# Two Strassen products taken together: the high halves of both weight blocks, then the low halves of both

## The chip, the core and the metric

The kernel runs on one core of a Trainium2 chip, as one launch. The metric is the device time of one execution in microseconds (us); lower is better. The engines are named as in the profile: PE is TensorE's matrix array and PEld its weight load, DVE is VectorE, ACT is ScalarE, POOL is GpSimd, SP is SyncE, which here only issues transfers.

## The reference

One layer of an encoder over 512 tokens and 2048 channels, in float32:

```python
u = rms_norm(h, mix_pre_g)
q, k, v, ca, cb, ga, gb = split(u @ w_in)
y_attn = neighbourhood_attention(q, k, v, rpb) @ w_attn_o
y_conv = conformer_conv(ca, cb, ...)
merged = sigmoid(ga) * y_attn + sigmoid(gb) * y_conv
h = h + rms_norm(merged @ w_out, mix_post_g)
u = rms_norm(h, ffn_pre_g)
gate, up = split(u @ w_gate_up)                     # 2048 -> 2 x 5632
h = h + rms_norm((silu(gate) * up) @ w_down, ffn_post_g)   # 5632 -> 2048
```

What matters here are four of its large matrix products: the two gates `ga` and `gb`, `merged @ w_out`, `u @ w_gate_up` and most of `... @ w_down`.

## The kernel before

**Precision.** PE works on rounded float32. A float32 operand is therefore split in two: `hi`, its rounded value, made by ACT (`halved_weights`, line 253), and `lo`, the rest, made by DVE (line 255). A product is the sum hi·hi + hi·lo + lo·hi. An activation block keeps its hi half (256 tokens) in columns A and its lo half in columns B of one 512-wide tile, so that hi weights times all 512 columns and lo weights times the 256 columns A are the three terms: for each product 8 matmuls of 512 columns, then 8 of 256 columns (8, because the inner size is 8 blocks of 128).

**Strassen.** `strassen()` makes two output tiles of 128 x 512 from 2 x 2 blocks with seven products in place of eight. Their operands on the weight side are blocks of the weights (a11, a12, a21, a22, loaded by `quarter`) and sums of them (s1 to s4; s1 is summed by an accumulating transfer from POOL's queue, s2 to s4 by DVE, `wsum`). Three accumulators in PSUM hold the sums: x, y and z. The order of the products on PE is:

1. x = a11 · "11"
2. y = s2 · "T2"
3. z = s1 · "T1"
4. y += s3 · "T3", after DVE has added the copy `p1` of x to y and ACT has copied y to `u2`
5. x += a12 · "21"
6. z += s4 · "22"
7. y += a22 · "T4"

In most calls products 4 and 6 take lo before hi (`turn`), so that runs of one width meet. `strassen()` is called 76 times: 14 calls for the gates (names g2 to g15), 7 for `w_out` (wo0 to wo12), 39 for `w_gate_up` (f5 to f43), and two rounds of 8 for `w_down` (d0 and d1; in the first of them `turn` is off). The first call of each group has `apart` set and puts product 5 into a bank of its own; the other 71 calls have not.

**What orders the work.** A scheduler places the instructions when the kernel is built and fixes one order for each engine; at run time an engine takes its instructions in that order, each waiting for its semaphores. Tiles come from pools that go round: the hi weights have 3 buffers (`whi`), the lo weights 3 (`wlo`). So the cast of the fourth product's hi weights waits until PE has read those of the first, the fifth those of the second, the sixth those of the third. The names in the trace are those of the calls: `g8h` and `g8l` are hi and lo weights of call g8, `g8q` a loaded block, `g8s` a sum, `g8v` the copies `p1`, `u2` and `p5` of PSUM banks (line 280), `g8c` the copies in `done` (line 298).

Some calls have other work beside them: in the `w_gate_up` calls POOL adds squares to a row (`row<-row,asq`, line 953) and scales stored tiles (line 975), in the `w_down` calls it scales outputs (line 1108).

Of the kernel before, what the change touches and what calls it, by code (L numbers as in the profile page):

```python
# [31 lines left out]
P = 128  # L32
NT = 512
# [38 lines left out]
def hybrid_block(ctx: ExitStack, tc, xT, vecs, rpb, mask, w_c0, w_qk, w_v, w_gg, w_cg, w_ao, w_co, w_out, w_g0, w_gu, w_dn, outT):  # L72
    nc = tc.nc
# [11 lines left out]
    HT, HN = KT // 2, NT // 2  # L85
    A, B = slice(0, HN), slice(HN, NT)

    def slot(name, dt=F32, shape=(P, NT)):
        return sp.tile(list(shape), dt, tag="slot", name=name)

    def bank(name):
        return mm.tile([P, NT], F32, tag="mm", name=name)
# [37 lines left out]
    def wraw(name):  # L130
        return wp.tile([P, 1024], F32, tag="raw", name=f"raw_{name}", bufs=5)
# [97 lines left out]
    def operands(b11, b2, t12, t34):  # L229
        return {  # L230
            "11": b11,
            **{n: [t[i] for t in b2] for i, n in enumerate(("21", "22"))},
            **{n: [t[i] for t in t12] for i, n in enumerate(("T1", "T2"))},
            **{n: [t[i] for t in t34] for i, n in enumerate(("T3", "T4"))},
        }

    def sums(w1, name, load=nc.sync.dma_start):

        s1 = stp.tile([P, 1024], F32, tag="S1", name=f"{name}s1")
        load(s1, w1[:, :1024])  # L240
        nc.gpsimd.dma_start(s1, w1[:, 1024:], accum_op=ALU.add)
        return s1

    def quarter(w, c, name, load=nc.sync.dma_start):

        raw = wp.tile([P, 1024], F32, tag="raw", name=f"{name}q", bufs=5)
        load(raw, w[:, c * 1024 : (c + 1) * 1024])
        return raw

    def halved_weights(w, name):  # L250

        hi = wp.tile([P, 1024], F32R, tag="whi", name=f"{name}h")
        nc.scalar.copy(hi, w)
        lo = wp.tile([P, 1024], F32R, tag="wlo", name=f"{name}l")
        nc.vector.tensor_tensor(out=lo, in0=w, in1=hi.bitcast(F32), op=ALU.subtract)
        return hi, lo

    def begun(w0, name):

        a11 = quarter(w0, 0, name)  # L260
        return (a11, *halved_weights(a11, name))

    def strassen(w0, w1, op, name, n, s1=None, behind_last=None, first=None, quarters=None, apart=False, turn=True):

        x, y, z = ((bank, abank)[n % 2](f"{name}_{i}") for i in range(3))

        def wsum(a, b, op, i):
            t = stp.tile([P, 1024], F32, tag="S", name=f"{name}s{i}")
            nc.vector.tensor_tensor(out=t, in0=a, in1=b, op=op)
            return t

        def copied(ps, i):
            t = stp.tile([P, NT], F32, tag="quad", name=f"{name}v{i}", bufs=3)
            nc.scalar.copy(t, ps)  # L280
            return t

        def product(ps, w, b, first=False, last=False, lo_first=False):
            hi, lo = w if isinstance(w, tuple) else halved_weights(w, name)
            ws = [slice(k * P, (k + 1) * P) for k in range(HT)]
            steps = [(hi, slice(0, NT)), (lo, A)]
            if lo_first:
                steps.reverse()
            for n, (wt, cols) in enumerate(steps):
                for k, t in enumerate(op[b]):  # L290
                    nc.tensor.matmul(
                        ps[:, cols], wt[:, ws[k]], t[:, cols], start=first and n + k == 0,
                        stop=last and n + k == HT, skip_group_check=True,
                    )

        def done(ps, i):
            t = stp.tile([P, HN], F32, tag="half", name=f"{name}c{i}", bufs=2)
            nc.scalar.copy(t, ps[:, B])
            return ps[:, A], t

        if quarters:
            a11, a12, a21, a22 = quarters
        elif apart:
            a11, a12, a21, a22 = (first[0], *(quarter(*w, name) for w in ((w0, 1), (w1, 0), (w1, 1))))
        s1 = s1 or sums(w1, name)
        if not apart:
            a11, a21, a12, a22 = (quarter(*w, name) for w in ((w0, 0), (w1, 0), (w0, 1), (w1, 1)))
        product(x, first[1:] if first else a11, "11", first=True)
        if apart:
            v = (bank, abank)[n % 2](f"{name}_3")  # L310
            product(v, a12, "21", first=True, last=True)
        s2 = wsum(s1, a11, ALU.subtract, 2)
        p1 = copied(x, 1)
        product(y, s2, "T2", first=True)
        product(z, s1, "T1", first=True)
        nc.vector.tensor_tensor(out=y, in0=y, in1=p1, op=ALU.add)
        u2 = copied(y, 2)
        s3 = wsum(a11, a21, ALU.subtract, 3)
        product(y, s3, "T3", lo_first=turn)
        p5 = copied(z, 3)  # L320
        nc.vector.tensor_tensor(out=z, in0=z, in1=u2, op=ALU.add)
        if apart:
            nc.vector.tensor_tensor(out=v, in0=v, in1=p1, op=ALU.add)
            x = v
        else:
            product(x, a12, "21", last=True)
        nc.vector.tensor_tensor(out=p5, in0=y, in1=p5, op=ALU.add)
        s4 = s2
        nc.vector.tensor_tensor(out=s4, in0=a12, in1=s2, op=ALU.subtract)
        c11 = done(x, 1)  # L330
        product(z, s4, "22", last=True, lo_first=turn)
        c12 = None if behind_last else done(z, 2)
        product(y, a22, "T4", last=True)
        if behind_last:
            behind_last()
            c12 = done(z, 2)
        return c11, c12, done(y, 3), (p5[:, A], p5[:, B])
# [240 lines left out]
    for h in range(H):  # L578
        bm = bias_of(h)
        qk = []  # L580
        for i in range(2):
            ps = bank(f"qk{h}_{i}")
# [86 lines left out]
    op = operands(b11, b2, t12, t34)  # L669
    for i in range(2, KT):  # L670
        if i > 2:
            s1, quarters = sums(w_cg[2 * CT + KT + 3], "g3", load_in_order) if i == 3 else None, None
        c11, c12, c21, c22 = strassen(
            w_cg[2 * CT + i], w_cg[2 * CT + KT + i], op, f"g{i}", i + 1, s1, quarters=quarters,
            apart=i == 2,
# [3 lines left out]
        if i == KT - 1:  # L679

            for h in range(0, H, 2):
                if h == H // 2:
                    first = wraw("y0_first")
# [106 lines left out]
    for i in (c + n * HT for c in range(HT) for n in range(2)):  # L790
        if i == KT - 1:
            first = begun(w_out[0], "wo0")
# [12 lines left out]
    op = operands(b11, b2, t12, t34)  # L805
    acc = None
    for i in range(0, KT - 2, 2):
        c11, c12, c21, c22 = strassen(
            w_out[i], w_out[i + 1], op, f"wo{i}", i // 2 + 1, first=None if i else first, apart=i == 0
        )  # L810
        for n, halves_of in enumerate((((A, c11), (B, c12)), ((B, c22), (A, c21)))):
            t = slot(f"fo{i + n}")
            for cols, c in halves_of:
                joined(t[:, cols], c)
            nc.scalar.dma_start(f_d[i + n], t)
            acc = sumsq(acc, t, f"f{i + n}")

    last = [slot(f"f{i}") for i in (KT - 2, KT - 1)]
# [3 lines left out]
    for i in range(0, HT, 4):  # L822
        t = stp.tile([P, 4, HN], F32, tag="S1", name=f"m12r{i}")
# [54 lines left out]
    for c in (*range(SPLIT), *range(HT)):  # L878
        if len(u) == 2 * c:
# [3 lines left out]
            cols = A if c < SPLIT else slice(0, NT)  # L883
        else:
            cols = B
# [20 lines left out]
    for j in range(3):  # L906
        t = stp.tile([P, 2, NT], F32, tag="S", name=f"sg{j}")
        t, up = t[:, 0], t[:, 1]
# [10 lines left out]
    for c in range(HT):  # L919
        hi, lo = wchunk(w_g0[1, c], f"f1_{c}")  # L920
        if c == HT - 1:
            first = begun(w_gu[5], "f5")
# [32 lines left out]
    for j in range(2):  # L955
        t = slot(f"sg{3 + j}")
# [5 lines left out]
    op = operands(b11, b2, b_t12, b_t34)  # L962
# [49 lines left out]
    for j in range(5, FT):  # L1012
        if j == FT - 2:
# [4 lines left out]
            first=first if j == 5 else None, apart=j == 5,  # L1018
# [13 lines left out]
        t, up = slot(f"sg{j}"), slot(f"su{j}")  # L1032
# [108 lines left out]
    y = [slot(f"y{o}") for o in range(KT)]  # L1141
# [55 lines left out]
    def halved(n, squares, pin=False):  # L1197

        r = []
        blocks = range(n * NB // 2, (n + 1) * NB // 2)  # L1200
        return (
            lambda: r.append(rstd(squares, D, f"r4{n}", blocks, pin)),
            lambda: r4.insert(0, by_column(r[0], f"r4{n}", blocks, pin)),
        )

    s1, s2 = halved(0, half(0), pin=True)
# [132 lines left out]
```

## Time and profile before

| | |
|---|---|
| median of 3 runs | 2496.39 us (2496.09 to 2500.19) |
| the profiled execution | 2495.9 us, of which the span from first to last instruction is 2494.1 us |
| PE busy | 2471.3 us of the span (99%) |
| DVE busy | 2078.5 us (83%) |
| ACT busy | 1251.1 us (50%) |
| POOL busy | 474.0 us (19%) |
| granted PE clock, mean | 0.997 of full speed |

In the rows of a timeline, matmuls that follow each other with one name are merged into one row: its start is that of the first, and "x8" their number. A PE row's length covers the last matmul's modelled end, which lies beyond the start of the next row; the time that a run takes on PE is therefore read from the start of one row to the start of the next.

### The profile page before, as it was taken

What the parts mean: (1) busy time and instruction counts of PE and PEld (TensorE: products, weight loads), DVE (VectorE), ACT (ScalarE), POOL (GpSimd) and SP (SyncE); (2) the same over time, 40 slices, a digit from 0 to 9 for tenths busy, and PEclk for the clock granted to TensorE, in tenths of its full rate; (3) what the DMA queues carried; (4) which work ended last, traced back from release to release, by engine and by line L of the source; (5) the groups of instructions that cost most, each with busy time, mean ns of one, the idle gap of its engine ahead of it and who ended that gap; (6) DMA issues with size and microseconds to landing.
All of it is one profiled execution on the core that took longest, in us unless ns stands there. A gap on an engine that the chain in (4) does not pass through costs nothing. (4 is left out here: it accounts for less than half of the span.)

```text
span 2494.1 us, 36076 instructions
## 1 busy us (share of the span) xinstructions
PE 2471.3 (99%) x13495; PEld 2147.5 (86%) x13495; DVE 2078.5 (83%) x2743; ACT 1251.1 (50%) x1939; POOL 474.0 (19%) x511
## 2 busy tenths in 40 slices
PE   9999999999999999999999999999999999999997
PEld 7888888888888888889998888888888888888887
DVE  5999897497777658878898888888888889989887
ACT  5223333365556424556455555555555565456553
POOL 0110132130000000021111111122222203532342
PEclk9999999999999999999999999999999999999998
DMA  5246332386667543669456665666666778888886
GB/s 208 96 141 203 106 107 97 117 265 193 195 191 222 179 158 129 201 210 306 141 169 173 182 182 165 184 197 201 213 207 188 226 229 237 240 229 255 225 222 195
DMA packets 165103, 472.89 MB, mean 190 GB/s; under 512 B 18752, under 2 KB 30656, under 8 KB 164928
## 3 DMA queue, kind: packets, MB, share of 16 engines
q1 hardware_dynamic: 109584, 334.02, 39.8%
q0 software_dynamic: 32928, 97.54, 18.2%
q10 hardware_dynamic: 22416, 39.04, 4.2%
q8 instruction: 106, 1.74, 0.3%
q14 instruction: 69, 0.57, 0.1%
HBM read 396.59 MB, written 71.30 MB: 188 GB/s over the span
## 5 line engine op out<-in xcount | busy, mean ns | idle before, releaser
L443 DVE SCALAR_TENSOR_TENSOR cv<-z,vec,cv 128x497 f32<-128x497 f32 (+14 forms) x240 | 190.6, 796 | 4.8
L953 POOL TENSOR_TENSOR row<-row,asq 128x512 f32<-128x512 f32 x30 | 54.1, 1805 | 397.3 <-ACT asq L952 397.3
L1108 POOL TENSOR_TENSOR ys<-ys,row 128x512 f32<-128x512 f32 x32 | 57.7, 1803 | 119.2 <-DVE ys L340 99.3
L143 ACT CAST whi_qk<-raw_qk 128x1024 fp32r<-128x1024 f32 x32 | 33.6, 1051 | 77.1 <-PE qk L193 56.5
L144 DVE TENSOR_TENSOR wlo_qk<-raw_qk,whi_qk 128x1024 fp32r<-128x1024 f32 x32 | 40.5, 1267 | 32.1 <-ACT whi_qk L143 31.9
L143 ACT CAST whi_y<-raw_y 128x1024 fp32r<-128x1024 f32 x31 | 32.6, 1051 | 64.8 <-PE py L193 52.7
L975 POOL TENSOR_TENSOR an<-an,row 128x512 f32<-128x512 f32 x32 | 50.4, 1576 | 74.6 <-DMA an<-a_d 48.5
L742 DVE TENSOR_TENSOR gg<-py,gg 128x512 f32<-128x512 f32 x32 | 21.9, 687 | 46.2 <-PE py L194 43.4
L190 PE MATMUL py<-ycl,whi_y 128*128 128x512 f32 x128 | 49.8, 389 | 0.0
L193 PE MATMUL py<-ych,whi_y 128*128 128x512 f32 x128 | 49.8, 389 | 0.0
L194 PE MATMUL py<-ych,wlo_y 128*128 128x512 f32 x128 | 49.8, 389 | 0.0
L524 POOL TENSOR_TENSOR bm<-braw,msk 128x128 f32<-128x128 f32 x56 | 42.6, 794 | 14.8 <-DMA braw<-in_rpb 14.8
L144 DVE TENSOR_TENSOR wlo_y<-raw_y,whi_y 128x1024 fp32r<-128x1024 f32 x31 | 37.8, 1223 | 9.1 <-ACT whi_y L143 8.7
L451 POOL TENSOR_TENSOR csum<-csum,cv 128x512 f32<-128x512 f32 x7 | 12.7, 1818 | 144.3 <-DVE cv L443 144.3
L173 PE MATMUL f<-b,whi_f 128*128 128x256 f32 x128 | 36.2, 283 | 0.0
L174 PE MATMUL f<-b,wlo_f 128*128 128x256 f32 x128 | 36.2, 283 | 0.0
L172 PE MATMUL f<-b,whi_f 128*128 128x256 f32 x128 | 36.2, 283 | 0.0
L143 ACT CAST whi_ca<-raw_ca 128x1024 fp32r<-128x1024 f32 x12 | 12.6, 1054 | 46.3 <-PE cb L193 18.1
L553 ACT ACTIVATE sc<-sc,st 128x256 f32<-128x256 f32 (+1 forms) x32 | 18.0, 563 | 33.1 <-DVE st L552 33.0
L1109 POOL DMA_DIRECT2D y_d<-ys x32 | 29.4, 919 | 9.4 <-POOL ys L1108 7.8
L769 POOL DMA_DIRECT2D m_d<-m x8 | 4.5, 557 | 136.7 <-ACT m L166 86.3
L575 POOL DMA_DIRECT2D att_d<-ao x8 | 4.4, 555 | 133.5 <-ACT ao L574 112.5
(3250 smaller groups left out, 8797.3 us busy)
## 6 DMA issues: line engine op xcount, KB each, us to landing
raw_qk<-in_w_qk SPq DMA_DIRECT2D x32, 512.0 KB, 3.6
raw_w<-in_w_dn SPq DMA_DIRECT2D x24, 512.0 KB, 5.5
a_d<-sg ACTq DMA_DIRECT2D x44, 256.0 KB, 4.2
raw_v<-in_w_v SPq DMA_DIRECT2D x16, 512.0 KB, 4.4
gg<-g_d SPq DMA_DIRECT2D x32, 256.0 KB, 4.2
raw_y<-in_w_co SPq DMA_DIRECT2D x16, 512.0 KB, 3.6
raw_f<-in_w_g SPq DMA_DIRECT2D x16, 512.0 KB, 4.1
an<-a_d POOLq DMA_DIRECT2D x32, 256.0 KB, 5.8
```

Of the source, the lines that this page charges most:

```text
L143: cast(hi[:, s], raw[:, s])
L144: nc.vector.tensor_tensor(out=lo[:, s], in0=raw[:, s], in1=hi[:, s].bitcast(F32), op=ALU.subtract)
L172: nc.tensor.matmul(o, hi, t[:, B], start=first, stop=False, skip_group_check=True)
L173: nc.tensor.matmul(o, hi, t[:, A], start=False, stop=False, skip_group_check=True)
L190: mmul = nc.tensor.matmul(ps, hi[:, s], al, start=first, stop=False)
L193: nc.tensor.matmul(ps, hi[:, s], ah, start=False, stop=False)
L194: nc.tensor.matmul(ps, lo[:, s], ah, start=False, stop=last)
L443: nc.vector.scalar_tensor_tensor(out=a[:, to], in0=z[:, fr], scalar=col(C_WDW, i * CW + w), in1=a[:, to], op0=ALU.mult, op1=ALU.add)
L524: nc.gpsimd.tensor_tensor(out=bm[:, o + i - i0], in0=raw[:, :, i * BC : (i + 1) * BC], in1=msk[:, o + i - i0, None, :].broadcast_to([P, RO ...
L953: nc.gpsimd.tensor_tensor(out=row[n], in0=row[n], in1=sq, op=ALU.add)
L975: ins = nc.gpsimd.dma_start(t, a_d[DN_P + k]), nc.gpsimd.tensor_tensor(out=t, in0=t, in1=row[k // KT], op=ALU.mult)
L1108: tc.keep_in_program_order(nc.gpsimd.tensor_tensor(out=t, in0=t, in1=row[n], op=ALU.mult))
```

## The change

In calls without `apart` the first two products are issued together: the 8 hi matmuls of x, the 8 hi matmuls of y, the 8 lo matmuls of x, the 8 lo matmuls of y. The copy `p1` of x stands behind them in the code. Nothing is added or left out, and calls with `apart` keep their order.

```diff
+        def half_product(ps, wt, b, cols, start=False, stop=False):
+
+            for k, t in enumerate(op[b]):
+                nc.tensor.matmul(
+                    ps[:, cols], wt[:, k * P : (k + 1) * P], t[:, cols], start=start and k == 0,
+                    stop=stop and k == HT - 1, skip_group_check=True,
+                )
...
-        product(x, first[1:] if first else a11, "11", first=True)
+        w11 = first[1:] if first else halved_weights(a11, name)
         if apart:
+            product(x, w11, "11", first=True)
             v = (bank, abank)[n % 2](f"{name}_3")
             product(v, a12, "21", first=True, last=True)
         s2 = wsum(s1, a11, ALU.subtract, 2)
-        p1 = copied(x, 1)
-        product(y, s2, "T2", first=True)
+        if apart:
+            p1 = copied(x, 1)
+            product(y, s2, "T2", first=True)
+        else:
+
+            wt2 = halved_weights(s2, name)
+            half_product(x, w11[0], "11", slice(0, NT), start=True)
+            half_product(y, wt2[0], "T2", slice(0, NT), start=True)
+            half_product(x, w11[1], "11", A)
+            half_product(y, wt2[1], "T2", A)
+            p1 = copied(x, 1)
         product(z, s1, "T1", first=True)
```

`product` itself now calls `half_product` twice, with the same matmuls as before.

The scheduler gives more than the code moves another place. The rows below are those of call g8; in them names carry numbers: `g8_0`, `g8_1` and `g8_2` are the accumulators x, y and z, `g8s1`, `g8s2` and `g8s3` the sums (s4 is written over s2), `g8v1` is p1, `g8v2` is u2, and `g8v3` is p5.

On PE, where product 3 (z, `g8_2`) ends and product 4 (y, `g8_1`, lo first) begins, before:

```order
3106 L291 MATMUL g8_2_5618<-t126_0_4439,g8l_5676 128x256
3107 L291 MATMUL g8_2_5618<-t127_0_4495,g8l_5676 128x256
3108 L291 MATMUL g8_1_5617<-t340_0_4109,g8l_5701 128x256
3109 L291 MATMUL g8_1_5617<-t341_0_4165,g8l_5701 128x256
3110 L291 MATMUL g8_1_5617<-t342_0_4221,g8l_5701 128x256
```

And with the change, at the same place on PE:

```order
3107 L286 MATMUL g8_2_5618<-t127_0_4495,g8l_5676 128x256
3108 L286 MATMUL g8_0_5616<-b20_0_4094,g8h_5722 128x512
3109 L286 MATMUL g8_0_5616<-b21_0_4150,g8h_5722 128x512
3110 L286 MATMUL g8_0_5616<-b22_0_4206,g8h_5722 128x512
3111 L286 MATMUL g8_1_5617<-t340_0_4109,g8l_5701 128x256
3112 L286 MATMUL g8_1_5617<-t341_0_4165,g8l_5701 128x256
```

Three of the eight hi matmuls of product 5 (x, `g8_0`) now stand between products 3 and 4; the other five follow product 4.

On ACT, from the cast of product 4's hi weights on, before:

```order
425 L253 CAST g8h_5699<-g8s3_5697 128x1024
426 L699 ACTIVATE gb7_5607<-gb7_5607 128x512
427 L280 COPY g8v1_5652<-g8_0_5616 128x512
428 L700 DMA g_d_4046<-gb7_5607 128x512
429 L253 CAST g8h_5722<-g8q_5626 128x1024
430 L280 COPY g8v2_5695<-g8_1_5617 128x512
431 L253 CAST g8h_5746<-g8s2_5650 128x1024
432 L280 COPY g8v3_5719<-g8_2_5618 128x512
```

And with the change, at the same place on ACT:

```order
425 L253 CAST g8h_5699<-g8s3_5697 128x1024
426 L712 ACTIVATE gb7_5607<-gb7_5607 128x512
427 L713 DMA g_d_4046<-gb7_5607 128x512
428 L253 CAST g8h_5722<-g8q_5626 128x1024
429 L280 COPY g8v1_5672<-g8_0_5616 128x512
430 L253 CAST g8h_5746<-g8s2_5634 128x1024
431 L280 COPY g8v2_5695<-g8_1_5617 128x512
432 L280 COPY g8v3_5719<-g8_2_5618 128x512
```

Two things moved: the copy p1 (`g8v1`) now stands behind the cast of a12, and the cast of s4 (`g8h` from `g8s2`) now stands ahead of the copy u2 (`g8v2`), where it stood behind it.

On DVE, from the lo weights of product 3 on, before:

```order
770 L255 TENSOR_TENSOR g8l_5676<-g8s1_5619,g8h_5674 128x1024
771 L340 TENSOR_TENSOR gb7_5607<-g7_1_5433,g7c3_5604 128x256
772 L255 TENSOR_TENSOR g8l_5701<-g8s3_5697,g8h_5699 128x1024
773 L275 TENSOR_TENSOR g9s2_5834<-g9s1_5803,g9q_5806 128x1024
774 L316 TENSOR_TENSOR g8_1_5617<-g8_1_5617,g8v1_5652 128x512
775 L255 TENSOR_TENSOR g8l_5724<-g8q_5626,g8h_5722 128x1024
776 L255 TENSOR_TENSOR g8l_5748<-g8s2_5650,g8h_5746 128x1024
```

And with the change, at the same place on DVE:

```order
770 L255 TENSOR_TENSOR g8l_5676<-g8s1_5619,g8h_5674 128x1024
771 L353 TENSOR_TENSOR gb7_5607<-g7_1_5433,g7c3_5604 128x256
772 L255 TENSOR_TENSOR g8l_5701<-g8s3_5697,g8h_5699 128x1024
773 L255 TENSOR_TENSOR g8l_5724<-g8q_5626,g8h_5722 128x1024
774 L329 TENSOR_TENSOR g8_1_5617<-g8_1_5617,g8v1_5672 128x512
775 L275 TENSOR_TENSOR g9s2_5818<-g9s1_5803,g9q_5806 128x1024
776 L255 TENSOR_TENSOR g8l_5748<-g8s2_5634,g8h_5746 128x1024
```

The lo weights of a12 (`g8l` from `g8q`) moved ahead of the addition y += p1, and the next call's s2 behind it.

Of the 71 calls without `apart`, 44 have these orders on PE and ACT: g3 to g15, wo2, f6 to f22 and f24 to f36. The other 27 (wo4 to wo12, f23, f37 to f43 and all of the d0 and d1 calls) keep u2 ahead of the cast of s4, and products 3 and 4 next to each other; on DVE they take the lo weights of s3, then y += p1, then the lo weights of a12. The orders of POOL's and SP's instructions are the same as before.

## Rows read from the trace of the kernel before

**Rows 1.** The page: share of the span of each engine, and PE's granted clock by slice.

```profile
span 2494.1 us, 36076 instructions
PE 2471.3 (99%) x13495; PEld 2147.5 (86%) x13495; DVE 2078.5 (83%) x2743; ACT 1251.1 (50%) x1939; POOL 474.0 (19%) x511
...
PEclk9999999999999999999999999999999999999998
```

**Rows 2.** Waits of PE: who waited for whom, us in total, times, longest.

```profile
PE py L194 <- DVE wlo_y L144: 1.5, 1, 1.5
PE r_b L367 <- POOL r_r L360: 1.3, 2, 1.0
...
PE g L291 <- DVE g L321: 0.7, 1, 0.7
```

**Rows 3.** Timeline of PE, call g8: start us, length us, engine, line, what.

```profile
649.20 2.00 PE L291 MATMUL g<-b,g8h 128*128 128x512 f32 x8
651.04 1.12 PE L291 MATMUL g<-b,g8l 128*128 128x256 f32 x8
652.00 2.00 PE L291 MATMUL g<-t,g8h 128*128 128x512 f32 x8
...
654.79 2.00 PE L291 MATMUL g<-t,g8h 128*128 128x512 f32 x8
656.63 2.08 PE L291 MATMUL g<-t,g8l 128*128 128x256 f32 x16
658.54 2.00 PE L291 MATMUL g<-t,g8h 128*128 128x512 f32 x8
660.38 1.98 PE L291 MATMUL g<-b,g8h 128*128 128x512 f32 x8
662.20 2.08 PE L291 MATMUL g<-b,g8l 128*128 128x256 f32 x16
...
668.72 0.63 PE L291 MATMUL g<-b,g9h 128*128 128x512 f32 x2
```

**Rows 4.** Timeline of PE, first `w_down` round: first run of two neighbouring calls.

```profile
2129.25 2.00 PE L291 MATMUL d<-d,d_6h 128*128 128x512 f32 x8
...
2148.81 0.40 PE L291 MATMUL d<-d,d_8h 128*128 128x512 f32 x1
```

**Rows 5.** Timeline of ACT and DVE in g8; in brackets idle time and its releaser.

```profile
646.90 1.05 ACT L253 CAST g8h<-g8s 128x1024 fp32r<-128x1024 f32 x1
...
655.06 0.70 DVE L316 TENSOR_TENSOR g<-g,g8v 128x512 f32<-128x512 f32 x1 [0.24 <-PE g L291]
...
655.79 0.59 ACT L280 COPY g8v<-g 128x512 f32<-128x512 f32 x1 [0.70 <-DVE g L316]
...
656.83 1.05 ACT L253 CAST g8h<-g8s 128x1024 fp32r<-128x1024 f32 x1 [0.45 <-PE g L291]
...
657.78 0.59 ACT L280 COPY g8v<-g 128x512 f32<-128x512 f32 x1
657.91 1.23 DVE L255 TENSOR_TENSOR g8l<-g8s,g8h 128x1024 fp32r<-128x1024 f32 x1 [1.03 <-ACT g8h L253]
...
659.05 0.69 DVE L321 TENSOR_TENSOR g<-g,g8v 128x512 f32<-128x512 f32 x1
```

**Rows 6.** Timeline of the first gate call, g2, where PE waits for u2.

```profile
540.91 0.69 DVE L316 TENSOR_TENSOR g<-g,g2v 128x512 f32<-128x512 f32 x1
...
541.63 0.59 ACT L280 COPY g2v<-g 128x512 f32<-128x512 f32 x1 [0.23 <-DVE g L316]
...
542.27 1.22 PE L291 MATMUL g<-t,g2l 128*128 128x256 f32 x8 [0.28 <-ACT g2v L280]
...
543.33 2.00 PE L291 MATMUL g<-t,g2h 128*128 128x512 f32 x8
```

**Rows 7.** Timeline of POOL and DVE in f10, and in f36.

```profile
1359.95 2.00 PE L291 MATMUL f<-b,f10h 128*128 128x512 f32 x8
...
1364.46 1.22 DVE L275 TENSOR_TENSOR f11s<-f11s,f11q 128x1024 f32<-128x1024 f32 x1
1364.48 2.36 POOL L953 TENSOR_TENSOR row<-row,asq 128x512 f32<-128x512 f32 x1 [15.75 <-ACT asq L952]
...
1873.60 1.29 POOL L953 TENSOR_TENSOR row<-row,asq 128x512 f32<-128x512 f32 x1 [12.81 <-ACT asq L952]
1873.64 2.32 DVE L275 TENSOR_TENSOR f37s<-f37s,f37q 128x1024 f32<-128x1024 f32 x1
```

More of the change, by code (lines that the diff above doesn't have):

```diff
@@ L281, in copied @@
             return t
+        def half_product(ps, wt, b, cols, start=False, stop=False):
[4 more added lines that the diff above has]
+                )
         def product(ps, w, b, first=False, last=False, lo_first=False):
             hi, lo = w if isinstance(w, tuple) else halved_weights(w, name)
-            ws = [slice(k * P, (k + 1) * P) for k in range(HT)]
             steps = [(hi, slice(0, NT)), (lo, A)]
@@ L289, in product @@
             for n, (wt, cols) in enumerate(steps):
[L290 to L294, printed above, removed]
+                half_product(ps, wt, b, cols, first and n == 0, last and n == 1)
         def done(ps, i):
```

## Prediction

> **What bounds the kernel now.** I read the page first: PE is busy for 99% of the span, at a granted clock of 2.4 GHz (9 in every slice but the last, which reads 8), while DVE has 83% and ACT 50% [rows 1]. A busy PE may still be a waiting one, so I read PE's waits next: the longest are single ones of 1.5 us, and inside the Strassen calls the largest is one of 0.7 us [rows 2]. PE's own order and pace therefore set the time. An edit gains only by making the matmuls follow each other faster, and loses by any wait that it brings to PE. In the 76 calls PE hardly waits, but what it does not wait for comes from a chain of DVE and ACT steps whose slack has to be read call by call.
>
> **What the regrouping itself is worth.** It moves matmuls and removes none. In g8 a run of eight hi matmuls takes 1.84 us behind a lo run (649.20 to 651.04) and 1.82 us behind another hi run (660.38 to 662.20); sixteen lo matmuls take 1.91 us, so eight take 0.95 to 0.96 [rows 3]. Entering a hi run from a lo run thus costs some 0.02 us. A second look gives the same: g8 enters a hi run five times and lasts 19.52 us from its first matmul to that of g9 [rows 3], d_6 in the first `w_down` round has the same matmuls, enters seven times and lasts 19.56 us [rows 4]; 0.04 us for two. One entry saved in all 71 calls would be 71 x 0.02 = 1.4 us, 0.06% of the time.
>
> But 44 of the 71 calls do not save it: there three hi matmuls of product 5 now stand between products 3 and 4, and the call enters a hi run five times as before. So the gain is 27 x 0.02 = **-0.5 us**.
>
> **What the other engines' order costs.** I follow g8 with T = 0 at its first matmul, and the durations of [rows 3]. x hi runs to 1.84, y hi (1.82) to 3.66, x lo to 4.61, y lo to 5.57, z hi (1.84) to 7.41, z lo to 8.36. The early need of y's hi weights is covered: the cast of s2 began at 646.90 and took 1.05 us, over a microsecond ahead of T = 0 [rows 5], and it is now needed at T = 1.84. The three filler matmuls of product 5 end at 8.36 + 3 x 0.23 = 9.05. Then comes product 4, which may write y only when ACT has copied it (u2).
>
> When is u2 done? The cast of s4 now stands ahead of it on ACT. That cast needs the buffer of z's hi weights, and so starts 0.20 us behind the start of z's lo run (656.63, 656.83 [rows 3, 5]): T = 7.41 + 0.20 = 7.61. The next ACT instruction starts 0.95 us later (656.83 to 657.78 [rows 5]): u2 at 8.56, with its 0.59 us done at 9.15. In g2, the one gate call where PE did wait for u2, PE went on 0.05 us after the copy's end (541.63 + 0.59 = 542.22, then 542.27 [rows 6]). So product 4 starts at 9.20 in place of 9.05: 0.15 us late. In g2 the eight lo matmuls after the wait took 1.06 us (542.27 to 543.33 [rows 6]) in place of 0.95, another 0.11. **0.26 us** for each call with this order. Queued behind the s4 cast is u2 alone, and behind u2 DVE's z += u2, which is needed by product 6 some 5 us later.
>
> Is u2's input ready by 8.56? DVE's lo weights of s3 now wait for x's lo run, which ends later. DVE follows the end of a PE run by 0.27 us (654.79, 655.06 [rows 3, 5]): 4.61 + 0.27 = 4.88. Lo weights take 1.14 us from their start to the next instruction's (657.91 to 659.05 [rows 5]): the lo weights of a12 at 6.02, the addition to y at 7.16, done at 7.86. That is 0.70 us early; it costs nothing in g3 to g15, wo2 and f21.
>
> In the other 29 of the 44 (f6 to f20, f22, f24 to f36) POOL adds a row of squares. In f10 that instruction starts at T = 1364.48 - 1359.95 = 4.53 [rows 7], 0.35 us before DVE's lo weights of s3 can now start. In f36 POOL was first by 0.04 us: it took 1.29 us, and DVE's instruction beside it 2.32 in place of 1.23, ending 1.07 us after POOL's [rows 7]. In f10 DVE was first by 0.02 us and POOL took 2.36 [rows 7]. So whoever comes second waits. Placing POOL at 4.53 to 5.82, the lo weights of s3 end at 5.82 + 1.07 = 6.89, as if begun at 5.66; a12's begin at 6.80, the addition at 7.94 and ends at 8.64. ACT follows by 0.03 us (540.91 + 0.69 = 541.60, then 541.63 [rows 6]): u2 at 8.67 in place of 8.56. **0.37 us** for each of these calls.
>
> The Trainium skill (SBUF — State Buffer, section "Who interferes with whom") has a rule that speaks against such a move: a VectorE instruction with two SBUF inputs and a GpSimd one that reads SBUF exclude each other, and the first to start blocks the other for its whole length. By that, taken strictly, the lo weights of s3 would begin at 5.82 rather than as if at 5.66, each of the 29 calls would lose 0.53 us, and the time would be 2515 us; the trace agrees on who waits, and I take its 1.07 us.
>
> In the 27 calls without filler u2 is ahead of the s4 cast: lo weights of s3 at 4.88, the addition at 6.02 to 6.72, u2 from 6.75 to 7.34, product 4 at 8.36. A microsecond of slack hides the later start, even with a POOL instruction of 1.29 us across most of it. Nothing is charged there, and a slip of 0.2 us in some of them would be a few microseconds at most.
>
> **The sum.** 15 x 0.26 + 29 x 0.37 - 0.5 = 3.9 + 10.7 - 0.5 = +14.1 us on the profiled execution's 2495.9 us (its span is 2494.1): **2510 us**. The median of the runs shown, 2496.39, is 0.5 us above that execution. Differences within 0.2%, 5 us, are about what a measurement here can't tell from no change.
>
> Bounds of what the rows of before don't show. The wait of 0.15 us is a difference of times that I trust to some 0.05 us, and the restart of 0.11 us is one example: with 0.10 and no restart, 44 x 0.10 - 0.5 = 3.9, or 2500 us. On the upper side DVE's lo weights of s3 could take the whole 2.32 us of f36 from 4.88: they end at 7.20, u2 starts at 8.98, 0.42 late, each of the 29 loses 0.68 us, and the sum is 19.7 + 3.9 - 0.5 = 23, or 2519 us.
>
> **The rivals.**
>
> *No wait at all (not slower).* If u2 ends by 9.00 in place of 9.15, the filler covers it, and what is left is the saved entries: 2495.4 us. It decides at 0.15 us, a sixth of the s4 cast that stands in front. For it: the margin is small, and three matmuls are in place to cover it. Against it: every step comes from a row of this kernel and the sum has no free term; POOL only makes it later. It would also be so if ACT could take u2 while the s4 cast waits; then u2 could run from 7.89 on. The Trainium skill (PSUM — Partial Sum Buffer, section "Engine vs sequencer instructions") says that ScalarE's queue is strictly first in, first out; no run here shows the opposite, so I leave this rival at 12%.
>
> *DVE is the bound in the f calls.* The forced pause until 4.88 costs DVE up to 1.5 us of each 19.5, at 83% busy on the mean [rows 1]. If POOL's other instructions also lengthen a12's lo weights by 1.09 us (2.32 - 1.23 [rows 7]) in the 14 later of these calls, u2 slips by about that much: 14 x 1.09 = 15 us more, 2525 us. It decides once the addition to y ends behind T = 8.53. For it: that margin is already used up in the sum. Against it: POOL works for 19% of the span [rows 1], and its queue holds the other instructions behind transfers. 15%.
>
> *The regrouping pays in all calls.* -1.4 us, 2494.5 us: it needs no wait and no filler, and even then stays below what can be told. 3% for anything faster by over 0.2%, this one included.
>
> **How the numbers follow.** The waits as summed have 70% (2502 to 2515), no wait 12%, DVE as bound 15%, faster 3%. Slower by over 0.2%: the first and third, with a little of the first lying below the bound and counted as same: 0.85. Within 0.2%: 0.12. Faster: 0.03. The range reaches from the lower bound to just above the upper one, 2500 to 2520 us, and leaves out most of rivals one and two and the faster case.
>
> **What would show it.** In the changed trace PE should wait about 0.15 to 0.3 us for ACT's copy, once in each of the 44 calls and at product 4, and the period of a g call should be 19.78 us in place of 19.52, that of f6 to f36 some 19.9. In wo4 to wo12, f37 to f43, d0 and d1 the period should be 0.02 us shorter and without a wait. The prediction is wrong if PE's waits at product 4 are missing, if they are released by DVE's lo weights of s3 rather than by the copy, or if waits turn up at products 6 or 7.

## The result and the profile after

The changed kernel takes **2509.49 us** (median of 6 runs, 2506.77 to 2510.40); the kernel before takes 2496.66 us beside it (6 runs, 2495.84 to 2500.19). The ratio is 1.0048, with a 95% interval of 1.0037 to 1.0058: slower by about 13 us, where 2510 was forecast.

The page of the profiled execution (2509.41 us), beside [rows 1]:

```profile
span 2507.6 us, 36110 instructions
...
PE 2481.1 (99%) x13495; PEld 2143.6 (85%) x13495; DVE 2063.3 (82%) x2743; ACT 1246.0 (50%) x1939; POOL 461.8 (18%) x511
...
PEclk9999999999999999999999999999999999999998
```

PE's busy time grew by 10 us and its share stayed at 99%: the page hides the waits, as the prediction warned ("A busy PE may still be a waiting one"). The clock is the same. The loss has to be read from starts.

The timeline of PE, DVE and ACT in g8, which answers to [rows 3, 5]; the call begins at 650.82, so T is the time less that. The copy row marked x2 holds u2 and, behind it, p5:

```profile
650.82 2.00 PE L286 MATMUL g<-b,g8h 128*128 128x512 f32 x8
...
654.47 1.11 PE L286 MATMUL g<-b,g8l 128*128 128x256 f32 x8
...
655.43 1.12 PE L286 MATMUL g<-t,g8l 128*128 128x256 f32 x8
655.70 1.23 DVE L255 TENSOR_TENSOR g8l<-g8s,g8h 128x1024 fp32r<-128x1024 f32 x1 [2.14 <-PE g L286]
...
657.98 0.69 DVE L329 TENSOR_TENSOR g<-g,g8v 128x512 f32<-128x512 f32 x1
...
658.23 1.12 PE L286 MATMUL g<-t,g8l 128*128 128x256 f32 x8
658.43 1.05 ACT L253 CAST g8h<-g8s 128x1024 fp32r<-128x1024 f32 x1 [2.06 <-PE g L286]
...
659.18 0.86 PE L286 MATMUL g<-b,g8h 128*128 128x512 f32 x3
659.39 1.06 ACT L280 COPY g8v<-g 128x512 f32<-128x512 f32 x2
...
660.01 1.00 PEld L286 LDWEIGHTS g<-t,g8l 128*128 128x128 f32 x8 [0.41 <-ACT g8v L280]
660.01 1.21 PE L286 MATMUL g<-t,g8l 128*128 128x256 f32 x8
...
661.06 1.32 PE L286 MATMUL g<-t,g8h 128*128 128x512 f32 x5
```

Step by step: z's lo run starts at T = 7.41, the cast of s4 at 7.61, u2 at 8.57. The filler starts at 8.36, and product 4 at 660.01, T = 9.19. Its lo run then takes 1.05 us (to 661.06) in place of 0.95. DVE's addition is done at 658.67, T = 7.85, 0.7 us ahead of the copy. PE's row shows no idle time ahead of product 4, but the row of its weight load does: PEld waited, and ACT's copy released it. DVE idles 2.14 us for x's lo run, which costs nothing here.

The timeline of f10, where POOL adds its row (answers to [rows 7]; T = 0 at 1364.89):

```profile
1364.89 2.00 PE L286 MATMUL f<-b,f10h 128*128 128x512 f32 x8
...
1369.42 1.29 POOL L966 TENSOR_TENSOR row<-row,asq 128x512 f32<-128x512 f32 x1 [16.16 <-ACT asq L965]
...
1369.77 2.03 DVE L255 TENSOR_TENSOR f10l<-f10s,f10h 128x1024 fp32r<-128x1024 f32 x1 [1.54 <-PE f L286]
...
1372.30 1.11 PE L286 MATMUL f<-t,f10l 128*128 128x256 f32 x8
1372.56 1.05 ACT L253 CAST f10h<-f10s 128x1024 fp32r<-128x1024 f32 x1 [1.86 <-PE f L286]
1372.86 0.69 DVE L329 TENSOR_TENSOR f<-f,f10v 128x512 f32<-128x512 f32 x1
...
1373.58 1.08 ACT L280 COPY f10v<-f 128x512 f32<-128x512 f32 x2
1374.22 1.21 PE L286 MATMUL f<-t,f10l 128*128 128x256 f32 x8
```

DVE's lo weights of s3, second to POOL, take 2.03 us and end 1.09 us behind it; the addition to y ends at T = 8.66, u2 starts at 8.69, product 4 at 9.33. But look at the cast: it starts 0.26 us behind z's lo run (1372.30), not 0.20 as in g8. Even with no POOL, ACT could not have taken u2 before T = 7.67 + 0.95 = 8.62, with the 0.95 us of [rows 5] from a cast's start to the next instruction's.

Periods (first matmul of a call to that of the next), as the difference between the two profiled executions; in us:

| calls | forecast per call | measured per call | forecast sum | measured sum |
|---|---|---|---|---|
| g3 to g15, wo2, f21 (15) | +0.26 | +0.22; f21 +0.28, g15 +0.25 | +3.9 | +3.4 |
| f6 to f20, f22 (16) | +0.37 | f7 to f20 +0.35 to +0.37, f6 +0.29, f8 +0.56, f22 +0.28 | +5.9 | +5.7 |
| f24 to f36 (13) | +0.37 | +0.29, f25 +0.34 | +4.8 | +3.9 |
| the other 27 | -0.02 | -0.02, with a few strays | -0.5 | -0.4 |

Together +12.6, of a span that is 13.5 us longer; calls with `apart` and the stretches between the groups hold the rest.

### The profile page after: what moved, and what is told of

The parts are those of the page before. It is cut to its first block, busy times and chain, and to the rows that moved or that the text cites. A ratio compares the mean times of both kernels' runs of the same rounds, so it can differ in the third digit from the quotient of the medians.

```text
span 2507.6 us, 36110 instructions
## 1 busy us (share of the span) xinstructions
PE 2481.1 (99%) x13495; PEld 2143.6 (85%) x13495; DVE 2063.3 (82%) x2743; ACT 1246.0 (50%) x1939; POOL 461.8 (18%) x511
## 5 line engine op out<-in xcount | busy, mean ns | idle before, releaser
L966 POOL TENSOR_TENSOR row<-row,asq 128x512 f32<-128x512 f32 x30 | 38.6, 1287 | 405.7 <-ACT asq L965 405.7
L143 ACT CAST whi_ca<-raw_ca 128x1024 fp32r<-128x1024 f32 x12 | 12.6, 1053 | 46.3 <-PE cb L193 18.1
L1051 DVE TENSOR_TENSOR sg<-sg,su 128x512 f32<-128x512 f32 x39 | 30.0, 770 | 0.0
```

The lines of the kernel that those rows point to most:

```text
L143: cast(hi[:, s], raw[:, s])
L966: nc.gpsimd.tensor_tensor(out=row[n], in0=row[n], in1=sq, op=ALU.add)
```

## The experiments

The state of things at this point: every call with the new ACT order loses at product 4, and the sizes are right within 0.1 us per call, but for f8. Two theories had to be told apart. **Mine:** two gates stand ahead of product 4. ACT's is the cast of s4, which waits for z's hi run and has u2 queued behind it; DVE's is the lo weights of s3, which wait for x's lo run and now have a12's lo weights ahead of the addition. The later one decides. **The rival:** only ACT's order matters, so putting u2 first again is the cure; or, the other way, the regrouping itself is the loss.

In the edits `issued_behind(a, b)` has the scheduler place instruction a behind instruction b on their engine. Lines that only keep the instructions by name, or set the same buffer count elsewhere, are left out ("..."). Rows of the first three experiments carry somewhat higher line numbers, since their kernels have a few lines more.

**1. u2 ahead of the cast again, in all 71 calls, nothing else.**

```diff
...
+        wt4 = halved_weights(s4, name)
+        if not apart:
+            issued_behind(casts[-1], copies[2])
-        product(z, s4, "22", last=True, lo_first=turn)
+        product(z, wt4, "22", last=True, lo_first=turn)
```

> The changed kernel with one edge added: ACT takes the copy u2 ahead of the cast of s4 in all calls, as before the change. DVE keeps the changed order (lo weights of a12 ahead of y += p1). In g4 to g14 the scheduler then puts products 3 and 4 next to each other, as in all f calls. Theory, two gates one behind the other (the s4 cast on ACT, and the late addition on DVE): the first gate is gone, the second now decides without a filler to cover it. The addition ended at T = 7.85 in g8 of the changed kernel, so u2 is done at 8.47, PE goes on at 8.52 in place of 8.36: 0.16 late, 0.1 for the restart, 0.02 saved, about +0.24 us on the period of before (19.51) in the g calls; in the 29 f calls with POOL's row addition the addition ends near 8.65, PE goes on near 9.3: about +1.0 us each. Sum about 12 x 0.24 + 29 x 1.0 = 32 us, some 2528 us. Rival, the s4 cast ahead of u2 is the only cause: all waits vanish, 2495 to 2496 us. Rival, the loss is in splitting product 5 on PE: the filler is gone here, so also 2495 to 2496 us.

Measured: 2530.67 us (4 runs; before 2496.97), ratio 1.0135 (1.0122 to 1.0149). Opening one gate made it worse by 21 us. The filler is gone, so product 4 is due at T = 8.36, and DVE's gate, which had been covered, is not. f10 (T = 0 at 1367.50):

```profile
1367.50 2.00 PE L288 MATMUL f<-b,f10h 128*128 128x512 f32 x8
...
1375.46 0.69 DVE L331 TENSOR_TENSOR f<-f,f10v 128x512 f32<-128x512 f32 x1
...
1376.24 0.59 ACT L282 COPY f10v<-f 128x512 f32<-128x512 f32 x1 [2.94 <-DVE f L331]
...
1376.87 1.22 PE L288 MATMUL f<-t,f10l 128*128 128x256 f32 x8 [0.85 <-ACT f10v L282]
```

ACT stood idle for 2.94 us waiting for DVE's addition (T = 7.96 to 8.65), PE for 0.85 us behind it. f6 to f20 and f24 to f36 lose 1.01 to 1.09 us each, the gate calls 0.29: there the addition ends at T = 7.85, the copy at 8.52.

**2. Both gates opened:** as experiment 1, and the addition to y ahead of a12's lo weights and of the next call's s2.

```diff
...
+        if not apart:
+            issued_behind(sums_of[2], adds[-1])
...
+            wt5 = halved_weights(a12, name)
+            issued_behind(lows[-1], added_y)
-            product(x, a12, "21", last=True)
+            product(x, wt5, "21", last=True)
...
```

> The changed kernel with both orders put back: on ACT u2 ahead of the s4 cast, on DVE y += p1 ahead of the lo weights of a12 and of the next call's s2, in all 71 calls. The regrouped hi and lo matmuls stay. Theory of two gates: with both open no wait is left (in the f calls u2 ends near T = 8.15, PE needs it at 8.36), and all 71 calls keep the saved entry of 0.02 us: 1.4 us under before, about 2495.2 us, period 19.49 us in g3 to g15, wo2 to wo12 and f6 to f43. Rival, the regrouping itself costs (x's lo buffer is released 1.8 us later, whatever the order): waits remain, and the time stays over 2500 us. Rival, the saved entry is worth nothing: 2496.5 us, period 19.51.

Measured: 2495.13 us (11 runs), ratio 0.9989 (0.9980 to 0.9998). All calls but a few strays have a period of 19.49 us, 0.02 less than before. f10 (T = 0 at 1358.96):

```profile
1358.96 2.00 PE L288 MATMUL f<-b,f10h 128*128 128x512 f32 x8
...
1363.49 1.28 POOL L976 TENSOR_TENSOR row<-row,asq 128x512 f32<-128x512 f32 x1 [15.81 <-ACT asq L975]
...
1363.84 2.02 DVE L257 TENSOR_TENSOR f10l<-f10s,f10h 128x1024 fp32r<-128x1024 f32 x1 [1.53 <-PE f L288]
...
1365.79 0.69 DVE L333 TENSOR_TENSOR f<-f,f10v 128x512 f32<-128x512 f32 x1
1366.37 2.08 PE L288 MATMUL f<-t,f10l 128*128 128x256 f32 x16
...
1366.51 0.59 ACT L282 COPY f10v<-f 128x512 f32<-128x512 f32 x1 [1.75 <-DVE f L333]
```

POOL delays DVE here exactly as in the changed kernel (2.02 us), and it costs nothing: the copy ends at T = 8.14, 0.22 us ahead of product 4, and the lo runs of products 3 and 4 are one run of 16. So the regrouping itself is not the loss; it gains what [rows 3, 4] said, 0.02 us per call. This is the best version, 0.11% faster than before, less than one can rely on.

**3. The kernel before, without the regrouping, with the cast of s4 ahead of u2 in all 71 calls.**

```diff
...
+        wt4 = halved_weights(s4, name)
+        if not apart:
+            issued_behind(copies[2], casts[-1])
-        product(z, s4, "22", last=True, lo_first=turn)
+        product(z, wt4, "22", last=True, lo_first=turn)
```

> The kernel before the change, with one edge added: ACT takes the cast of s4 ahead of the copy u2 in all 71 calls. Products 1 and 2 are not regrouped, and DVE adds p1 to y early, as before. The scheduler puts three matmuls of product 5 between products 3 and 4 here too. Theory: the s4 cast ahead of u2 is enough for the wait by itself, whatever the order of products 1 and 2: product 3's lo run starts at T = 7.43, the cast at 7.63, u2 at 8.58 and done at 9.17, PE goes on at 9.22 in place of 9.07 behind the three matmuls; with the restart and one more entry into a hi run about +0.24 us in each of 71 calls, and no more in the f calls than in the g calls, since DVE is early: +17 us, about 2513 us. Rival, the regrouping (the late lo buffer) is the cause and the order on ACT only goes with it: no wait, 2496 to 2498 us.

Measured: 2518.25 us (4 runs), ratio 1.0083 (1.0067 to 1.0098), +21.3 us summed over the periods, of which 1.6 stand in the first call of the second `w_down` round, whose ACT order the edit does not touch. Gate calls lose 0.25, f calls 0.29 to 0.31, whether POOL adds in them or not, most others 0.26 to 0.31. ACT's order alone makes the loss, filler included, in calls that the change left alone too; I had put the price of the f calls 0.06 too low. g8 (T = 0 at 650.44):

```profile
650.44 2.00 PE L293 MATMUL g<-b,g8h 128*128 128x512 f32 x8
...
656.30 0.70 DVE L318 TENSOR_TENSOR g<-g,g8v 128x512 f32<-128x512 f32 x1 [0.24 <-PE g L293]
...
658.07 1.05 ACT L255 CAST g8h<-g8s 128x1024 fp32r<-128x1024 f32 x1 [1.74 <-PE g L293]
658.82 0.86 PE L293 MATMUL g<-b,g8h 128*128 128x512 f32 x3
659.02 1.07 ACT L282 COPY g8v<-g 128x512 f32<-128x512 f32 x2
...
659.66 1.22 PE L293 MATMUL g<-t,g8l 128*128 128x256 f32 x8
```

Cast at T = 7.63, u2 at 8.58, product 4 at 9.22: the changed kernel's picture, without its regrouping. DVE's addition is done at 6.56 here, long before ACT comes to u2, so DVE's gate has no part in it.

**4. The change without POOL's row addition.** It leaves out the addition of the squares to the rows, and with them their sums.

```diff
-                nc.gpsimd.tensor_tensor(out=row[n], in0=row[n], in1=sq, op=ALU.add)
```

> The changed kernel without POOL's additions of squares to the two rows in the w_gate_up calls (the rows then hold one square each; ACT still makes the squares). Orders on PE, ACT and DVE stay as in the changed kernel. Theory: the excess of the f calls over the g calls (0.35 in f7 to f20 and 0.29 in f24 to f36, against 0.22 in g4 to g14, all over the periods of before) is POOL's instruction standing before DVE's lo weights of s3; without it the f calls fall to +0.22: 14 x 0.13 + 13 x 0.07 and a little for f8, about 3 us less, 2506 to 2507 us. Rival, the excess comes from ACT's square or its transfer issue ahead of the a12 cast: the periods of the f calls stay at +0.29 to +0.35, 2509 us.

Measured: 2507.87 us (4 runs), ratio 1.0042 (1.0028 to 1.0056). f7 to f20 fall from +0.35 to +0.28 or +0.29 (f8 stays at +0.56); f24 to f36 stay at +0.27 to +0.29. I expected +0.22 in all of them, as in the gate calls: half wrong. f25 falls from +0.34 to +0.29. So POOL costs 0.05 to 0.08 us in 14 calls (f7, f9 to f20 and f25), 1 us in all, and at most 0.02 us in each of the others. This is read from the periods; the two medians, 1.6 us apart, would not show it by themselves. What keeps the f calls 0.07 above the gate calls is the cast's later start on ACT, which was in this trace and in the one of before, and which I had not looked at in an f call.

**5. The change with four buffers for the hi weights in place of three** (and 64 in place of 66 slots for other tiles). Is it the order on ACT, or what the cast in front waits for?

```diff
...
-        hi = wp.tile([P, 1024], F32R, tag="whi", name=f"{name}h")
+        hi = wp.tile([P, 1024], F32R, tag="whi", name=f"{name}h", bufs=4)
...
```

> The change with 4 buffers in place of 3 for the hi weights (and 64 in place of 66 slots for other tiles, to make room). The cast of s4 still stands ahead of u2 on ACT in all calls, and ahead of p1 too, but it now needs the buffer of y's hi weights, free at T = 3.65, in place of z's, free at 7.41. No filler stands between products 3 and 4 except in g3 and g15, and DVE adds p1 to y ahead of the lo weights of a12. My theory (the price is the wait of that cast for its buffer, with everything behind it on ACT, not the order of the names): the cast runs from about 3.9 to 4.9, the addition ends at 6.7 (7.5 beside POOL), u2 by 8.2, product 4 starts at 8.36 unhindered, every call is 0.02 us shorter than before the change: 2495 us. Rival (a cast ahead of the copy always costs, or POOL's row of squares makes the addition too late by itself): 0.2 to 0.3 us in each call or in the 29 calls with POOL's addition, 2502 to 2512 us.

Measured: 2497.86 us (10 runs; before 2496.28), ratio 1.0003 (0.9993 to 1.0013). 62 of the 71 calls, f7 to f36 with it but for f23, have a period 0.02 us shorter than before. f10 (T = 0 at 1361.86):

```profile
1361.86 2.00 PE L286 MATMUL f<-b,f10h 128*128 128x512 f32 x8
...
1365.71 1.05 ACT L253 CAST f10h<-f10s 128x1024 fp32r<-128x1024 f32 x1 [0.23 <-PE f L286]
...
1367.94 0.69 DVE L329 TENSOR_TENSOR f<-f,f10v 128x512 f32<-128x512 f32 x1
...
1368.65 0.59 ACT L280 COPY f10v<-f 128x512 f32<-128x512 f32 x1 [1.40 <-DVE f L329]
1369.27 2.08 PE L286 MATMUL f<-t,f10l 128*128 128x256 f32 x16
```

The cast of s4 is still ahead of u2, but runs at T = 3.85, behind y's hi run, and product 4 follows product 3 at once. So a cast in front of the copy costs nothing by itself; with experiment 3, the price is the wait of that cast for its buffer. The buffer moved DVE's order too: the addition now stands ahead of a12's lo weights, so this run opens both gates, as experiment 2 does by hand. The time missed its 2495 us outside these calls. In the profiled execution PE is 0.5 us behind the kernel before at 184 us of that kernel's span and 3.7 us behind at 233 us, in the matrix product `pv`, ahead of all Strassen calls; experiment 7, which has the 64 slots alone, loses nothing there. Why that happens with the fourth buffer is open.

**6. The change with four buffers for the lo weights** (and 64 slots).

```diff
...
-        lo = wp.tile([P, 1024], F32R, tag="wlo", name=f"{name}l")
+        lo = wp.tile([P, 1024], F32R, tag="wlo", name=f"{name}l", bufs=4)
...
```

> The change with 4 buffers in place of 3 for the lo weights (and 64 in place of 66 slots for other tiles). DVE's lo weights of s3 no longer wait for x's lo run; those of a12 do. In the gate and w_out calls the scheduler now puts u2 ahead of the cast of s4: 0.02 us shorter than before the change. In f6 to f22, f24 to f36 and one more the cast stays ahead of u2, with the filler, and the lo weights of a12 ahead of the addition. My theory: there ACT's gate alone decides, with its cast at T = 7.66, and POOL costs nothing: +0.29 us in each, also in f7 to f20, where the change costs 0.35; 31 x 0.29 - 40 x 0.02 = +8 us, 2505 us. Rival (POOL's row of squares still delays DVE's addition by blocking the lo weights of a12 in place of those of s3): +0.35 in f7 to f20, 2506 us; rival (DVE's pause until 4.88 was the cause of it all): -0.02 in all calls, 2495 us.

Measured: 2521.60 us (4 runs), ratio 1.0099 (1.0084 to 1.0114). In the calls that it was meant for it went as expected: g3 to g15 -0.02, f6 to f22 and f24 to f36 +0.27 to +0.30 with no difference between early and late ones (f19 strayed to +0.57, and wo2, where the cast stayed in front, lost 0.23). f10 (T = 0 at 1361.99):

```profile
1366.52 2.35 POOL L966 TENSOR_TENSOR row<-row,asq 128x512 f32<-128x512 f32 x1 [16.04 <-ACT asq L965]
...
1367.64 2.32 DVE L255 TENSOR_TENSOR f10l<-f10q,f10h 128x1024 fp32r<-128x1024 f32 x1
...
1369.65 1.05 ACT L253 CAST f10h<-f10s 128x1024 fp32r<-128x1024 f32 x1 [1.86 <-PE f L286]
1369.88 0.69 DVE L329 TENSOR_TENSOR f<-f,f10v 128x512 f32<-128x512 f32 x1
...
1370.61 1.07 ACT L280 COPY f10v<-f 128x512 f32<-128x512 f32 x2
1371.24 1.22 PE L286 MATMUL f<-t,f10l 128*128 128x256 f32 x8
```

The addition ends at T = 8.58, u2 starts at 8.62, as ACT's cast allows: POOL makes DVE wait by a microsecond and the call loses 0.29 all the same. What I did not expect are the `w_down` calls, +0.96 to +1.09 in 11 of the 14 without `apart`, 11.4 us of the miss; f23, f39 and f42 add 3.2. There u2 stands ahead of the cast, no filler covers, and DVE has the next call's s2 and a12's lo weights ahead of the addition: the pattern of experiment 1. That order is not enough by itself. g3 to g15, f40 and f41 of this run have it too and keep -0.02: in f40 the addition ends at T = 7.48. What the losing calls have besides is a POOL instruction that lengthens one of DVE's ahead of the addition by about 1 us. d_6 of the first round (T = 0 at 2144.42):

```profile
2148.57 1.63 POOL L1121 TENSOR_TENSOR ys<-ys,row 128x512 f32<-128x512 f32 x1
2148.80 2.48 DVE L275 TENSOR_TENSOR d_8s<-d_8s,d_8q 128x1024 f32<-128x1024 f32 x1
...
2151.21 1.21 DVE L255 TENSOR_TENSOR d_6l<-d_6q,d_6h 128x1024 fp32r<-128x1024 f32 x1
...
2152.34 0.68 DVE L329 TENSOR_TENSOR d<-d,d_6v 128x512 f32<-128x512 f32 x1
2153.06 0.59 ACT L280 COPY d_6v<-d 128x512 f32<-128x512 f32 x1 [3.25 <-DVE d L329]
...
2153.70 2.12 PE L286 MATMUL d<-d,d_6h 128*128 128x512 f32 x8 [0.76 <-ACT d_6v L280]
```

The next call's s2 takes 2.48 us behind POOL's instruction, where it takes 1.23 in g8 of this run, and the addition ends at T = 8.60, u2 is done at 9.23 and product 4 starts at 9.28, where it was due at 8.36.

**7. The kernel before with 64 slots**, the control of experiments 5 and 6.

```diff
-    sp = ctx.enter_context(tc.tile_pool(name="sp", bufs=66))
+    sp = ctx.enter_context(tc.tile_pool(name="sp", bufs=64))
```

> The kernel before with 64 in place of 66 slots for other tiles, as in the two runs with a fourth buffer, to see what the two slots are worth by themselves. Expected: no change, 2496.5 us, all periods as before within 0.02 us. Rival: loads start later and PE waits for them here and there, some us more; then the two other runs have to be read against this one.

Measured: 2499.86 us (10 runs), ratio 1.0012 (1.0003 to 1.0021): the rival, not the expectation. The Strassen calls without `apart` keep their periods; g2, wo0 and d_0 of the second round, the first of their groups, are 1.6 to 2.1 us longer, though g2 also begins 1.3 us earlier, and the last of the three strays in other runs too (see the end). Against this control experiment 5 is 2.0 us faster by the medians; since it loses its time at another place, that difference is not the gain of the calls.

## Why the prediction was right, point by point

**The saved entries** were right: -0.02 us per call wherever nothing waits, 19.513 to 19.493 us, in 22 of the 26 calls whose period can be read, and in nearly all 71 of experiment 2.

**ACT's order** was right step by step. Forecast for g8: cast 7.61, u2 8.56, product 4 at 9.20. Measured: 7.61, 8.57, 9.19. The restart, taken from the one example in [rows 6] as 0.11, is 0.10 (1.05 us for the lo run in place of 0.95). The term of 0.26 us came out at 0.22 by the period. The unrounded starts of g8's matmuls place it: 0.135 us of wait and 0.097 of restart, less 0.013, since the three filler matmuls pay less for entering a hi run (0.017 us) than the eight would have (0.028); the sum is 0.219, so splitting product 5 costs nothing beyond the wait and the restart. Experiments 3 and 5 show that the wait of the cast is the cause: the order on ACT alone, without the regrouping, brings the loss, and with an earlier buffer the cast may stay in front, once DVE is early as well. The Trainium skill (PSUM — Partial Sum Buffer, section "Engine vs sequencer instructions") has ScalarE take its instructions strictly in order. The trace agrees in experiment 3: in g8 the input of u2 was ready at T = 6.56, ACT stood idle until 7.63, and u2 still started only at 8.58, behind the cast. In the changed kernel g8 can't tell: its cast had begun at 7.61, before u2's input was ready at 7.85. So the prediction's other way out, u2 running from 7.89 while the cast waits, was not one: by its own times the cast no longer waited then, and held ACT until 8.56.

**POOL's term is the one that was mis-sized**, with the right sum for a partly wrong reason. The step "ACT follows by 0.03 us: u2 at 8.67 in place of 8.56. 0.37 us for each of these calls" gave POOL 0.11 us in 29 calls, 3.2 us. The times were right (u2 at T = 8.69, product 4 at 9.33 in f10), but 8.56 was the wrong time to compare with: in an f call the cast starts 0.26 us behind z's lo run, not 0.20, so u2 could not have begun before 8.62. Of the 0.11, then, some 0.06 is ACT's in all 30 f calls with this order, f21 too, and 0.07 POOL's in f7, f9 to f20 and f25 alone; that makes some 2.8 us in place of 3.2, and that it comes so near is luck. In the others of f24 to f36 POOL's addition begins some 0.07 us earlier (T = 4.46 in f30 against 4.53 in f10), and the addition ends in time for ACT: nothing. The cast's 0.25 us stood in the trace of f10 before the change; I had read it in g8 only.

**DVE behind POOL.** The forecast end of s3's lo weights, T = 6.89, is 6.91 in f10. The Trainium skill (SBUF — State Buffer, section "Who interferes with whom") has the second of the two blocked for the whole length of the first. On who waits the trace agrees; on how long it differs: DVE ended 1.09 us behind POOL's end where it takes 1.23 alone, so the sum by the strict rule, 2515 us, was too high.

**The 27 calls** were right: a microsecond of slack hid the later lo weights, but for a stray of +0.15 us in d_4 of the first `w_down` round and the saved entry that f23 does not show.

**The rivals.** No wait at all fell: product 4 starts 0.14 us behind the filler's end in the gate calls, 0.2 in most of f24 to f36 and 0.27 in f10, and later than that end in all 44. DVE as the bound fell for this kernel, but DVE's gate and ACT's lie within some 0.07 us of each other in the f calls where POOL's row comes first; experiment 1 shows what stands behind it, 1.0 us per call, as soon as ACT's gate and the filler are gone. In the `w_down` calls of experiment 6 the rival's mechanism is seen at work: POOL lengthens a DVE instruction by about 1 us, the addition slips, and the call loses as much. That the regrouping pays in all calls is true of experiment 2, where both orders were put right, and it then pays about what the prediction said, 0.02 us per call.

**What would show it.** The periods did, and so does the list of waits of the weight loads (PEld): in each of the 44 calls product 4's first weight load waits for u2's copy, 0.41 us in the gate calls, 0.46 to 0.54 in the f calls, 0.74 in f8. In the trace of before only g2, f5 and d_0 of the second round have such a wait. These times count from the end of the weight load before, and so are longer than what PE lost. The list of PE's own waits shows little: the modelled end of the filler's last matmul covers most of the wait, and of the 44 I found a row in f8 alone, which lost most:

```profile
1334.48 1.22 PE L286 MATMUL f<-t,f8l 128*128 128x256 f32 x8 [0.31 <-ACT f8v L280]
```

So "PE should wait about 0.15 to 0.3 us, once in each of the 44 calls" is right in fact; the place to read it is PEld, not PE.

## What to carry to other kernels

Before a regrouping on the engine that bounds is priced by its own matmuls, look at when each tile's buffer now comes free and what the scheduler does on the other engines with that: here 0.02 us per call was to be had and 0.2 to 0.37 was lost to a cast that stood in front of a copy and waited for its buffer. Several gates can stand ahead of one matmul, and only the last shows as a wait, so price the second before opening the first: undoing one alone cost 21 us more, undoing both gave the gain. Read each step's delay in one call of every group, not in one call for all, and look for short waits of PE in the rows of its weight loads.

## What the runs showed of the hardware that I had not expected

- **A cast with one more semaphore instruction ahead of it starts later.** The cast of s4 waits for PE's semaphore alone in g8, and for PE's and one of ACT's own in f10; the trace has one more semaphore instruction on ACT's queue there. The cast starts 0.20 us behind the start of z's lo run in g8 and 0.26 in f10, and the same stands in the trace of before, 0.20 [rows 3, 5] and 0.25 (f10, 1367.38 to 1367.63). The Trainium skill (Perfetto Trace Analysis, section "Identifying Dependency Chains") says that an instruction which waits for several engines may have semaphore instructions put ahead of it, and the trace agrees. No run varied the wait alone, so that it is the cause of the 0.06 us is argued, not shown. The rows of f10 before the change:

```profile
1367.38 2.08 PE L291 MATMUL f<-t,f10l 128*128 128x256 f32 x16
...
1367.63 1.05 ACT L253 CAST f10h<-f10s 128x1024 fp32r<-128x1024 f32 x1 [0.50 <-PE f L291]
```

- **f8** has that extra instruction at the same T = 7.61, and its cast only at 7.94, 0.28 later than in f10, both in the changed kernel and, by its +0.56, in experiment 4. What delays it is open.
- **The first call of the second `w_down` round** differs from that of before by -0.5 to +1.6 us from profile to profile, without a relation to the edits that I can see; that is open too, and is one reason not to read differences of 1 us from a single time.
